# A hybrid decoder layer on one core: prompt scores in three split passes, square sums in two, two zero-fills dropped

## The chip, the cores and the metric

One core of one Trainium2 chip runs the whole layer as one program. The metric is device time in microseconds of one execution, as the median over executions. A program's executions differ a little, so two medians less than about 0.5% apart can't be told from no change here.

## What is computed

One inference step of one decoder layer (D_MODEL 2048) serves a prompt of 512 tokens and a sample group of 8 x 4 tokens with the same weights. Both groups stand side by side as 544 columns of the activations.

```
h = RMSNorm(x);  z = h @ W_in
branch A: sparse attention: compressed blocks, selected blocks, sliding window; 8 heads, 2 K/V groups
branch B: multi-scale causal pooling
branch C: Mamba-2 scan (16 heads of 64, state 128, chunks of 128), y * SiLU(z), then
          yg = yg * rsqrt(mean(yg*yg) + EPS)   over 2 groups of 512 channels
merge:    x + W_out( sum_b sigmoid(G_b) * (m_b @ W_branch_b) )
```

For the prompt, the selected-block and the window branch both see all earlier tokens (512 tokens are 8 selection blocks of 64, fewer than the 16 that are chosen, and the window is 512). So each is an ordinary causal softmax attention: scores `q k^T`, a causal mask, softmax, and a product with V. Everything is held in float32.

## The kernel before, in words

**Two ways of multiplying.** A plain float32 product is issued by the program as one call and runs as two instruction pairs (a weight load and a matmul, twice). The large projections instead split both operands into a rounded part `hi` and a remainder `lo`, both of the type float32r (`hsplit`, line 494: ScalarE writes `hi`, VectorE writes `lo`), and add three products, `hi*hi + lo*hi + hi*lo`. A float32r product runs as one instruction pair. All matmuls go through `mm` (L153), all ScalarE operations through `act` (L173), most of VectorE's through `tt`, `ts`, `stt` (L176, L181 and L182, L185), so the rows are told apart by their tiles' names.

**Units and sides.** `run_units` (line 462) goes through a list of units. A unit is a quarter of the contraction of one 128-column block of a projection: 24 float32r matmuls of 272 columns into the tile `zin`. With each unit it issues the weight loads of the unit six ahead and splits (`wh` on ScalarE, `wl` on VectorE) the weights of the unit three ahead. After each unit a counter decides whether the side work makes one step (0.55 steps per unit, later 0.75). Side work is a set of generators: attention, scan, norms. Below this program order a scheduler of the framework fixes the order on each engine by what is ready, so side matmuls stand between the matmuls of units.

**Tiles.** Most data tiles come from one pool, `U` (line 140), of 32 tiles of 128x608 float32. A tile goes back when the program lets go of it and its last reader is done. PSUM has four one-bank tiles (`A`, line 143) for side work and two pairs of banks for `zin`.

**Prompt attention**, `attn_p` (line 769), runs once for each K/V group g, one after the other, in the stretch from 396 to 718 us. It has 32 items (4 heads x 4 query blocks x 2 branches), two per step, in three stages that lag by a step each: `sa` (line 812) makes the scores of query block i against (i+1) x 128 keys, adds the causal mask on the last 128 columns by a bf16 product with the identity, and takes the softmax on VectorE and ScalarE (tile `P`); `sb` transposes P (tile `PT`, written back by VectorE or ScalarE in turn); `sc` multiplies with V (tile `O`). The 4 query tiles and the 2 key tiles of the group are let go at the end (lines 862 to 865).

**The scan**, `ssd` (line 1142), goes over 4 chunks. For each, `out(k)` (line 1183, k from 0 to 3) fills one PSUM tile `y` of two 128-column blocks e: a bf16 product of zeros (`zb`) over all 256 columns, then four heads (two per block, each on 64 of the 128 partitions; two instructions each), then for each block, from the second chunk on, the part that comes from the state (`yo`, two instructions), then a VectorE operation that reads the block.

**The group norm of the scan**, `m_norm` (line 1347), makes for each of 2 groups four tiles `mz`: it loads the gate, multiplies (VectorE) and squares (ScalarE). Then a product of an all-ones matrix with the four tiles sums over partitions into `ms`, in two halves of 272 columns, in plain float32: 8 products, 16 instruction pairs per group.

**Sample attention**, `samp_group` (line 1639): `begin` (line 1703) starts the tile `sO` with a bf16 product of zeros and adds the product of the new keys (`nt`, `vn`). It is called 8 times.

Of the kernel before, what the change touches and what calls it, by code (L numbers as in the profile page):

```python
# [8 lines left out]
R = mybir.dt.float32r  # L9
# [9 lines left out]
T = 544  # L19
NP = 512  # L20
H = 272
# [102 lines left out]
class Prog:  # L124
# [644 lines left out]
    def attn_p(s, g):  # L769
        nc = s.nc  # L770
        while not s.kv_done or s.turn != g:
            yield
        q = [s.qT[g * 4 + e] for e in range(4)]
        p = s.A("cs")
        for e in range(4):
            s.mm(p[32 * e:32 * e + 32, :NP], s.kcp[:, 32 * g:32 * g + 32], q[e][:, :NP])
        st = s.U("cst")
        s.act(st[:, :NP], p)
        yield
        p = s.A("ct")  # L780
        for i in range(4):
            s.tr(p[:, i * 128:i * 128 + 128], st[:, i * 128:i * 128 + 128])
        E = s.U("cE")
        e4 = E[:, :NP].rearrange("p (i h b) -> p i h b", i=4, h=4)
        s.tt(e4, p.rearrange("p (i h b) -> p i h b", i=4, h=4),
             s.c("cmpneg").rearrange("p (i b) -> p i b", i=4)[:, :, None, :].to_broadcast([128, 4, 4, 32]), OP.add)
        e3 = E[:, :NP].rearrange("p (x b) -> p x b", b=32)
        mx = s.small(16)
        nc.vector.tensor_reduce(mx, e3, axis=AX.X, op=OP.max)
        s.ts(mx, mx, -1e29, OP.max)  # L790
        s.tt(e3, e3, mx[:, :, None].to_broadcast([128, 16, 32]), OP.subtract)
        s.act(E[:, :NP], E[:, :NP], AF.Exp, scale=SC)
        yield
        sm = s.small(16)
        nc.vector.tensor_reduce(sm, e3, axis=AX.X, op=OP.add)
        s.ts(sm, sm, 1e-30, OP.max)
        nc.vector.reciprocal(sm, sm)
        gv = s.gn.rearrange("p i (h b) -> p i h b", b=3)
        s.tt(sm.rearrange("p (i h) -> p i h", i=4), sm.rearrange("p (i h) -> p i h", i=4),
             gv[:, :, g * 4:g * 4 + 4, 0])  # L800
        s.tt(e3, e3, sm[:, :, None].to_broadcast([128, 16, 32]))
        yield
        p = s.A("cpt")
        for i in range(4):
            s.tr(p[:, i * 128:i * 128 + 128], E[:, i * 128:i * 128 + 128])
        pc = s.U("pc")
        s.act(pc[:, :NP], p)
        yield
        us = [(e, br, i) for e in range(4) for i in range(4) for br in range(2)]
        PP, PT, OO = {}, {}, {}  # L810

        def sa(n):
            e, br, i = us[n]
            L = i * 128 + 128
            S = s.A("S")
            s.mm(S[:, :L], q[e][:, i * 128:L], s.kv[4 + 4 * br + g][:, :L], True, False)
            s.mm(S[:, L - 128:L], s.identb, s.trib, False, True)
            mx, sm = s.small(1), s.small(1)
            nc.vector.tensor_reduce(mx, S[:, :L], axis=AX.X, op=OP.max)
            s.ts(mx, mx, -1e29, OP.max, -SC, OP.mult)  # L820
            P = s.U("P")
            s.act(P[:, :L], S[:, :L], AF.Exp, bias=mx, scale=SC, accum_out=sm)
            s.ts(sm, sm, 1e-30, OP.max)
            nc.vector.reciprocal(sm, sm)
            c = (g * 4 + e) * 3 + 1 + br
            s.ts(P[:, :L], P[:, :L], sm, OP.mult, s.gn[:, i, c:c + 1], OP.mult)
            PP[n] = P

        def sb(n):
            i = us[n][2]  # L830
            P = PP.pop(n)
            L = i * 128 + 128
            t = s.A("PT")
            for kt in range(i + 1):
                s.tr(t[:, kt * 128:kt * 128 + 128], P[:, kt * 128:kt * 128 + 128])
            PT[n] = s.U("PT")
            if n % 2:
                s.act(PT[n][:, :L], t[:, :L])
            else:
                nc.vector.tensor_copy(PT[n][:, :L], t[:, :L])  # L840

        def sc(n):
            e, br, i = us[n]
            pt = PT.pop(n)
            if n % 8 == 0:
                OO[e] = s.A("O")
                s.mm(OO[e][:, :NP], s.vc4[32 * e:32 * e + 32, g], pc[32 * e:32 * e + 32, :NP], True, False,
                     skip_group_check=True)
            for kt in range(i + 1):
                s.mm(OO[e][:, i * 128:i * 128 + 128], s.Vn[kt][:, br * 256 + g * 128:br * 256 + g * 128 + 128],  # L850
                     pt[:, kt * 128:kt * 128 + 128], False, br == 1 and kt == i, skip_group_check=True)
            if n % 8 == 7:
                o = s.U("Os")
                s.act(o[:, :NP], OO.pop(e))
                nc.sync.dma_start(s.oT[g * 4 + e][:, :NP], o[:, :NP])
        for n in range(0, 36, 2):
            for f, d in ((sc, 4), (sb, 2), (sa, 0)):
                for m in (n - d, n - d + 1):
                    if 0 <= m < 32:
                        f(m)  # L860
            yield
        for e in range(4):
            del s.qT[g * 4 + e]
        for br in range(2):
            del s.kv[4 + 4 * br + g]
        s.turn = g + 1


# [273 lines left out]
    def ssd(s):  # L1142
        nc, a = s.nc, s.a
# [4 lines left out]
        for c in range(4):  # L1148
            cs = slice(c * 128, c * 128 + 128)
            xd, yo = [], []  # L1150
            for g in range(2):
                p = s.A("xn")
# [5 lines left out]
            p = s.A("bn")  # L1158
# [24 lines left out]
            def out(k):  # L1183
                E = ES.pop(k)
                g = k // 2
                p = s.A("y")
                s.mm(p[:, :256], s.zb[:, :128], s.zb, True, False, skip_group_check=True)
                for e in range(4):
                    x0 = ((k % 2) * 4 + e) * 64
                    s.mm(p[64 * (e % 2):64 * (e % 2) + 64, (e // 2) * 128:(e // 2) * 128 + 128], xd[g][:, x0:x0 + 64],  # L1190
                         E[:, e * 128:e * 128 + 128], False, c == 0, skip_group_check=True)
                for e in range(2):
                    if c:
                        x0 = ((k % 2) * 2 + e) * 128
                        s.mm(p[:, e * 128:e * 128 + 128], yo[g][:, x0:x0 + 128], s.c("ident"), False, True,
                             skip_group_check=True)
                    t = 2 * k + e
                    s.stt(s.xb[t][:, cs], s.xb[t][:, cs], s.dsk[:, t:t + 1], p[:, e * 128:e * 128 + 128],
                          OP.mult, OP.add)
# [3 lines left out]
            if c:  # L1203
                for g in range(2):
                    p = s.A("yo")
# [14 lines left out]
            for g in range(2):  # L1220
                s.tt(s.h64(xd[g][:, :NP]), s.h64(xd[g][:, :NP]), s.hb(s.dte[:, c, g * 8:g * 8 + 8]))
                p = s.A("st")
# [8 lines left out]
        for g in range(2):  # L1231
            p = s.A("fs")
# [114 lines left out]
    def m_norm(s):  # L1347
        nc = s.nc
        for t in range(8, 12):
            del s.xb[t]  # L1350
        for g in range(2):
            Z = []
            for e in range(4):
                y = s.xb[g * 4 + e]
                z = s.U("mz")
                nc.sync.dma_start(z[:, :T], s.mzd[g * 4 + e])
                s.tt(y[:, :T], y[:, :T], z[:, :T])
                s.act(z[:, :T], y[:, :T], AF.Square)
                Z.append(z)
            yield  # L1360
            P = [s.A("ms") for _ in range(2)]
            for e, z in enumerate(Z):
                for hf in range(2):
                    s.mm(P[hf][:, :H], s.c("ones"), z[:, hf * H:hf * H + H], e == 0, e == 3)
            del Z, z
            ss, rs, tmp = s.U("mss"), s.U("mrs"), s.U("mt")
            for hf in range(2):
                nc.vector.tensor_copy(ss[:, hf * H:hf * H + H], P[hf][:, :H])
            s.rsqrt(rs[:, :T], ss[:, :T], 0.25 / 512, tmp[:, :T])
            yield  # L1370
            for e in range(4):
                t = g * 4 + e
                y = s.xb.pop(t)
                s.stt(y[:, :T], y[:, :T], s.mnh[:, t:t + 1], rs[:, :T])
                nc.sync.dma_start(s.brd[16 + t], y[:, :T])
            yield
# [262 lines left out]
    def samp_group(s, q, oc, cnt, os_, CI, need):  # L1639
        nc, a = s.nc, s.a  # L1640
# [3 lines left out]
        for bl in range(2):  # L1644
            dst = a["o_win_s"][0, 2 * q + bl].rearrange("t k g d -> t (k g d)")
            for e in range(4):
                lo = 4 if e == 0 else 0
                nc.sync.dma_start(dst[e * 128 + lo - 4:e * 128 + 124], wn[bl, e][0][lo:, :NP])
        vn = s.U("vn")
# [3 lines left out]
        p = s.A("bq")  # L1653
        ql = s.qs[:, q].rearrange("p c w -> p (c w)")
# [47 lines left out]

        def begin(br, nt):
            po = s.A("sO")
            s.mm(po[:, :128], s.zb[:, :128], s.zb[:, :128], True, False, skip_group_check=True)
            s.mm(po[:, :128], nt[:16, :128], vn[:16, br * 128:br * 128 + 128], False, False, skip_group_check=True)
            return po

        def sums(po, pt, raw, o, last):
# [10 lines left out]
        p = s.A("vn")  # L1720
# [3 lines left out]
        p = scores(kT)  # L1724
# [10 lines left out]
        S = []  # L1735
        for lq in range(4):
            p = scores(kT)
# [20 lines left out]
        nt = news(0)  # L1758
# [282 lines left out]
```

## Time and profile before

| | |
|---|---|
| runs before | 2399.49 us median of 3 (2393.22 to 2402.33) |
| the profiled execution's own time | 2404.53 us |
| its span | 2402.8 us |
| instructions | 48653 |

The span is the time from the first to the last record of the profiled execution. Its own time is larger by 1.73 us, which lies around the span. Times within the trace are counted from the start of the span. In rows of the timeline the first number is the start, the second the length of the row; a matmul's length includes its way through the array, so what a matmul costs in a full queue is read from the start of one to the start of the next.

### The profile page before, as it was taken

How to read it: one execution, taken by the hardware profiler on the slowest of the kernel's cores; microseconds unless marked ns; L12 is line 12 of the kernel's file. 1: busy time of each engine (PE TensorE's matmuls, PEld its weight loads, DVE VectorE, ACT ScalarE, POOL GpSimd, SP SyncE). 2: the span in 40 equal slices, each digit the busy share in tenths (PEclk: the TensorE clock that was granted, in tenths of full speed). 3: DMA queues.
4: the chain of work that ended last, by engine and by line, in shares of the span. 5: the costliest groups of instructions: out<-in, count | busy, mean ns of one | idle time of the engine just before them, and what ended most of it. 6: DMA issues, size and time to landing. Idle time of an engine off the chain costs nothing.

```text
span 2402.8 us, 48653 instructions
## 1 busy us (share of the span) xinstructions
PE 2370.6 (99%) x19842; PEld 2247.1 (94%) x19842; DVE 1088.2 (45%) x2204; ACT 723.1 (30%) x1374; POOL 64.5 (3%) x157
## 2 busy tenths in 40 slices
PE   6999999999999999999999999999999999999999
PEld 6999898999999999989899989988899999999999
DVE  4326657554543322324544565665463344445222
ACT  4222323333333222322433342322242322223221
POOL 0001011000000000000001000000000000000000
PEclk8999999999999999999999999999999999999999
DMA  5775755545439798886587763345555654443442
GB/s 143 204 206 148 207 148 153 148 141 164 120 114 279 226 283 234 250 248 179 159 257 238 220 203 85 107 120 148 161 184 153 193 153 138 131 130 102 132 124 83
DMA packets 541201, 409.49 MB, mean 170 GB/s; under 512 B 26673, under 2 KB 472409, under 8 KB 540978
## 3 DMA queue, kind: packets, MB, share of 16 engines
q1 hardware_dynamic: 534066, 393.01, 56.4%
q10 hardware_dynamic: 6912, 13.37, 1.5%
q8 instruction: 156, 2.56, 0.5%
q14 instruction: 67, 0.55, 0.1%
HBM read 360.56 MB, written 113.21 MB: 197 GB/s over the span
## 4 chain that ended last, share of the span: by engine, by line
PE 94%; DVE 2%; DMA 2%; issue 1%; ACT 0%; POOL 0%; SPq 0%; DVEq 0%; ACTq 0%
PE zin L153 74%; PE kT L156 3%; PE O L153 2%; PE S L153 2%; PE xT L153 1%; PE y L153 1%; PE sO L153 1%; PE sS L153 1%; PE PT L156 1%; PE cS L153 1%; PE ns L153 1%; PE ocT L153 1%; DMA kr<-ckd 1%; PE qw L153 1%; DVE rp L176 1%
## 5 line engine op out<-in xcount | busy, mean ns | idle before, releaser
L176 DVE TENSOR_TENSOR wl<-wr,wh 128x512 fp32r<-128x512 f32 (+1 forms) x612 | 424.5, 694 | 889.6 <-ACT wh L173 887.6
L153 PE MATMUL zin<-hhi,wh 128*128 128x272 f32 (+2 forms) x3616 | 774.5, 294 | 0.0
L153 PE MATMUL zin<-hhi,wl 128*128 128x272 f32 (+2 forms) x3616 | 756.2, 289 | 4.3 <-DVE wl L176 4.3
L153 PE MATMUL zin<-hlo,wh 128*128 128x272 f32 (+2 forms) x3616 | 756.4, 290 | 0.0
L173 ACT ACTIVATE wh<-wr 128x512 fp32r<-128x512 f32 (+1 forms) x612 | 384.6, 628 | 1098.2 <-PE zin L153 1016.1
L153 PEld LDWEIGHTS zin<-hhi,wh 128*128 128x128 f32 (+1 forms) x3616 | 568.7, 188 | 24.1 <-issue 20.1
L153 PEld LDWEIGHTS zin<-hhi,wl 128*128 128x128 f32 (+1 forms) x3616 | 570.9, 189 | 8.3 <-DVE wl L176 5.0
L153 PEld LDWEIGHTS zin<-hlo,wh 128*128 128x128 f32 (+1 forms) x3616 | 567.7, 189 | 4.4 <-issue 3.5
L153 PE MATMUL zin<-bh,wh 128*128 128x272 f32 x1280 | 266.1, 289 | 1.5 <-DVE gt L185 1.5
L153 PE MATMUL zin<-bh,wl 128*128 128x272 f32 x1280 | 265.2, 288 | 0.0
L153 PE MATMUL zin<-bl,wh 128*128 128x272 f32 x1280 | 264.9, 288 | 0.0
L153 PEld LDWEIGHTS zin<-bh,wh 128*128 128x128 f32 x1280 | 200.3, 188 | 1.9 <-ACT bh L173 1.7
L153 PEld LDWEIGHTS zin<-bh,wl 128*128 128x128 f32 x1280 | 200.6, 188 | 0.0
L153 PEld LDWEIGHTS zin<-bl,wh 128*128 128x128 f32 x1280 | 200.4, 188 | 0.0
L156 PEld LDWEIGHTS kT<-cst,kr 128*128 128x128 f32 x512 | 55.7, 141 | 11.7 <-issue 10.1
L156 PE MATMUL kT<-cst,kr 128*128 128x128 f32 x512 | 65.1, 277 | 0.0
L173 ACT ACTIVATE mg<-zin 128x544 f32<-128x544 f32 x48 | 29.9, 624 | 112.8 <-PE zin L153 110.2
L173 ACT ACTIVATE kT<-kT 128x512 f32<-128x512 f32 x72 | 42.7, 596 | 55.8 <-PE kT L156 55.1
L1445 DVE COPY kT<-kT 128x512 f32<-128x512 f32 x72 | 48.2, 688 | 5.0 <-PE kT L156 4.6
L185 DVE SCALAR_TENSOR_TENSOR gt<-gt,zin 128x544 f32<-128x544 f32 x32 | 23.1, 721 | 48.1 <-PE zin L153 46.4
L173 ACT ACTIVATE P<-S,sm 128x128 f32<-128x128 f32 (+3 forms) x64 | 33.8, 528 | 36.8 <-DVE sm L182 22.8
L153 PE MATMUL S<-kv,q 128*128 128x128 f32 (+3 forms) x128 | 44.3, 450 | 0.0
(414 smaller groups left out, 1857.3 us busy)
## 6 DMA issues: line engine op xcount, KB each, us to landing
wr<-in_w_in_dram SPq DMA_DIRECT2D x224, 512.0 KB
ckd<-in_cache_kv_dram SPq DMA_DIRECT2D x256, 256.0 KB
kr<-ckd SPq DMA_DIRECT2D x256, 256.0 KB
wr<-in_w_branch_dram SPq DMA_DIRECT2D x48, 512.0 KB
wr<-in_w_out_dram SPq DMA_DIRECT2D x32, 512.0 KB
mgd<-mg ACTq DMA_DIRECT2D x48, 272.0 KB
gt<-mgd SPq DMA_DIRECT2D x48, 272.0 KB
cw<-in_cmp_w_dram SPq DMA_DIRECT2D x48, 256.0 KB
```

The lines of the kernel that those rows point to most:

```text
L153: return s.nc.tensor.matmul(out, l, r, start=start, stop=stop, **kw)
L156: return s.nc.tensor.transpose(out, in_, s.c("ident")[:k, :k])
L173: return s.nc.scalar.activation(out, in_, f, **kw)
L176: return (eng or s.nc.vector).tensor_tensor(out, a, b, op=op)
L185: return s.nc.vector.scalar_tensor_tensor(out, a, sc, b, op0=op0, op1=op1)
L1445: s.nc.vector.tensor_copy(u[:, :NP], p)
```

## The change

The prompt's scores are made by three products of split operands. `halves` splits a tile into `hi` and `lo` (two new tiles of the pool), and the unsplit tile is let go: both key tiles of the group and the first query tile ahead of the first item, each further query tile one step before its head's first item. In the scan the product of zeros goes, and the first head's product of each block half starts the sum; the order becomes two heads, state part, read, for each block. In the group norm the squares are split, the ones matrix is copied to float32r once, and the sums are made by two products (`hi` and `lo`). In the sample attention the product of zeros goes.

```diff
@@ attn_p
+        K, Q = {}, {}
+
+        def halves(v):
+            hi, lo = s.U("sh").bitcast(R), s.U("sl").bitcast(R)
+            s.hsplit(v[:, :NP], hi[:, :NP], lo[:, :NP])
+            return hi, lo
+
+        def query(e):
+            Q[e] = halves(s.qT.pop(g * 4 + e))
+        for br in range(2):
+            K[br] = halves(s.kv.pop(4 + 4 * br + g))
+        query(0)
 
         def sa(n):
             e, br, i = us[n]
             L = i * 128 + 128
             S = s.A("S")
-            s.mm(S[:, :L], q[e][:, i * 128:L], s.kv[4 + 4 * br + g][:, :L], True, False)
+            (qh, ql), (kh, kl) = Q[e], K[br]
+            for n_, (a_, b_) in enumerate(((qh, kh), (ql, kh), (qh, kl))):
+                s.mm(S[:, :L], a_[:, i * 128:L], b_[:, :L], n_ == 0, False)
             s.mm(S[:, L - 128:L], s.identb, s.trib, False, True)
...
+        q = None
         for n in range(0, 36, 2):
+            if n % 8 == 0 and 0 < n < 32:
+                Q.pop(n // 8 - 1)
+            if n % 8 == 6 and n < 24:
+                query(n // 8 + 1)
             for f, d in ((sc, 4), (sb, 2), (sa, 0)):
...
             yield
-        for e in range(4):
-            del s.qT[g * 4 + e]
-        for br in range(2):
-            del s.kv[4 + 4 * br + g]
         s.turn = g + 1
@@ ssd, out(k)
                 p = s.A("y")
-                s.mm(p[:, :256], s.zb[:, :128], s.zb, True, False, skip_group_check=True)
-                for e in range(4):
-                    x0 = ((k % 2) * 4 + e) * 64
-                    s.mm(p[64 * (e % 2):64 * (e % 2) + 64, (e // 2) * 128:(e // 2) * 128 + 128], xd[g][:, x0:x0 + 64],
-                         E[:, e * 128:e * 128 + 128], False, c == 0, skip_group_check=True)
                 for e in range(2):
+                    for e_ in (2 * e, 2 * e + 1):
+                        x0 = ((k % 2) * 4 + e_) * 64
+                        s.mm(p[64 * (e_ % 2):64 * (e_ % 2) + 64, e * 128:e * 128 + 128], xd[g][:, x0:x0 + 64],
+                             E[:, e_ * 128:e_ * 128 + 128], True, c == 0, skip_group_check=True)
                     if c:
                         x0 = ((k % 2) * 2 + e) * 128
                         s.mm(p[:, e * 128:e * 128 + 128], yo[g][:, x0:x0 + 128], s.c("ident"), False, True,
@@ m_norm
                 s.act(z[:, :T], y[:, :T], AF.Square)
-                Z.append(z)
+                hi, lo = s.U("mzh").bitcast(R), s.U("mzl").bitcast(R)
+                s.hsplit(z[:, :T], hi[:, :T], lo[:, :T])
+                Z.append((hi, lo))
+            hi = lo = z = None
+            if g == 0:
+                on = s.U("on").bitcast(R)
+                nc.vector.tensor_copy(on[:, :128], s.c("ones"))
             yield
             P = [s.A("ms") for _ in range(2)]
-            for e, z in enumerate(Z):
+            for e in range(4):
                 for hf in range(2):
-                    s.mm(P[hf][:, :H], s.c("ones"), z[:, hf * H:hf * H + H], e == 0, e == 3)
-            del Z, z
+                    for j in range(2):
+                        s.mm(P[hf][:, :H], on[:, :128], Z[e][j][:, hf * H:hf * H + H], e == 0 and j == 0, e == 3 and j == 1)
+            Z = None
@@ samp_group, begin
             po = s.A("sO")
-            s.mm(po[:, :128], s.zb[:, :128], s.zb[:, :128], True, False, skip_group_check=True)
-            s.mm(po[:, :128], nt[:16, :128], vn[:16, br * 128:br * 128 + 128], False, False, skip_group_check=True)
+            s.mm(po[:, :128], nt[:16, :128], vn[:16, br * 128:br * 128 + 128], True, False, skip_group_check=True)
             return po
```

## Rows read from the trace of the kernel before

**Rows 1.** The page, busy time and share of the span of each engine.
```profile
PE 2370.6 (99%) x19842; PEld 2247.1 (94%) x19842; DVE 1088.2 (45%) x2204; ACT 723.1 (30%) x1374; POOL 64.5 (3%) x157
```

**Rows 2.** Waits of PE over the whole run, the longest: total, times, longest.
```profile
PE xT L153 <- DVE dg L181: 12.3, 3, 8.2
```

**Rows 3.** Windows: length, busy PE, PEld, DVE, ACT, POOL, clock, DMA; attention group 0, scan.
```profile
396.00:550.00 154.00, 152.97 (x1141) 138.98 (x1140) 80.99 (x223) 54.09 (x126) 3.02 (x3) 1.00 0.48 139
...
1550.00:1645.00 95.00, 95.00 (x725) 82.06 (x724) 64.10 (x159) 23.89 (x42) 1.02 (x3) 1.00 0.38 104
```

**Rows 4.** The tile S, matmuls of the scores: ns min/median/max, first and last start.
```profile
L153 PE MATMUL S<-kv,q x128: 272/460/649, 397.0 to 703.2; 128*128 128x128 f32 x32, 128*128 128x256 f32 x32, 128*128 128x384 f32 x32, 128*128 128x512 f32 x32
```

**Rows 5.** Timeline of PE: scores of 512 and of 128 columns, with what follows.
```profile
454.88 1.02 PE L153 MATMUL S<-kv,q 128*128 128x512 f32 x2
455.74 0.22 PE L153 MATMUL S<-trib,identb 128*128 128x128 bf16 x1
...
465.04 0.39 PE L153 MATMUL S<-kv,q 128*128 128x128 f32 x2
465.26 0.22 PE L153 MATMUL S<-trib,identb 128*128 128x128 bf16 x1
```

**Rows 6.** Timeline of PE: float32r products of 256 columns at the start.
```profile
22.04 0.28 PE L153 MATMUL zin<-hhi,wh 128*128 128x256 f32 x1
...
22.97 0.28 PE L153 MATMUL zin<-hlo,wh 128*128 128x256 f32 x1
```

**Rows 7.** The chain that ended last: a stretch of float32r products of 272 columns.
```profile
2375.31 12.05 PE zin L153 x96
```

**Rows 8.** Timeline of PE: twelve float32 instructions of 128 columns in a row.
```profile
462.83 1.50 PE L153 MATMUL O<-PT,Vn 128*128 128x128 f32 x12
464.16 1.04 PE L156 MATMUL PT<-cst,P 128*128 128x128 f32 x8
```

**Rows 9.** Timeline of PE: the group norm's sums and the unit behind them.
```profile
1738.45 3.83 PE L153 MATMUL ms<-mz,cst 128*128 128x272 f32 x16
...
1742.36 0.41 PE L153 MATMUL zin<-hhi,wl 128*128 128x272 f32 x2
```

**Rows 10.** Timeline of PE: the sample attention's sO started.
```profile
1165.39 0.23 PE L153 MATMUL sO<-zb 128*128 128x128 bf16 x1
1165.55 0.48 PE L153 MATMUL sO<-vn,nT 16*128 16x128 f32 x2
```

**Rows 11.** Timeline of PE: the scan's y, in the first and the second chunk.
```profile
1552.89 0.28 PE L153 MATMUL y<-zb 128*128 128x256 bf16 x1
1553.10 0.66 PE L153 MATMUL y<-E,xd 128*64 128x128 f32 x8
1553.69 0.28 PE L153 MATMUL y<-zb 128*128 128x256 bf16 x1
...
1578.27 0.49 PE L153 MATMUL y<-cst,yo 128*128 128x128 f32 x2
1578.69 0.43 PE L153 MATMUL y<-E,xd 128*64 128x128 f32 x2
1579.05 0.49 PE L153 MATMUL y<-cst,yo 128*128 128x128 f32 x2
1579.29 0.50 PE L153 MATMUL zin<-hhi,wh 128*128 128x272 f32 x2
```

**Rows 12.** Timeline of PEld (weight loads) in the same place, idle before it in brackets.
```profile
1579.05 0.30 PEld L153 LDWEIGHTS y<-cst,yo 128*128 128x128 f32 x2 [0.17 <-issue]
```

**Rows 13.** Splits of a 128x512 tile, by line and form: count, busy, mean ns, idle before.
```profile
L173 ACT ACTIVATE wh<-wr 128x512 fp32r<-128x512 f32 x608 | 383.1, 630 | 1091.0 <-PE zin L153 1010.8 <-issue 72.9 <-DMA ckd<-in_cache_kv_dram 2.4
L176 DVE TENSOR_TENSOR wl<-wr,wh 128x512 fp32r<-128x512 f32 x608 | 423.0, 697 | 879.6 <-ACT wh L173 877.6 <-DMA wr<-in_w_in_dram 1.3
```

**Rows 14.** Timeline of PE: the first scores of group 0 and their first transpose.
```profile
396.96 0.38 PE L153 MATMUL S<-kv,q 128*128 128x128 f32 x2
...
402.30 0.33 PE L156 MATMUL PT<-cst,P 128*128 128x128 f32 x1 [1.01 <-DVE sm L181]
```

## The prediction

> **What bounds the kernel now.** I read the page first: PE is busy for 2370.6 of 2402.8 us, VectorE for 45% and ScalarE for 30% [rows 1]. Then PE's waits: the longest entry is 12.3 us in the opening, where the change does nothing [rows 2]. Then the busy time of the stretches that the change touches. In the attention of group 0 (that of group 1 is alike) and in the scan PE is busy for all but 1 us, at a granted clock of 1.00, while VectorE has about half of the attention free and a third of the scan, and ScalarE two thirds or more [rows 3]. So the time is the length of PE's queue. What an edit is worth is how much earlier the next matmul starts, and work on other engines costs only what it makes PE wait for. A matmul's own length in a row is no measure of that; starts are.
>
> **The prices of a pass.** A float32 score product of 512 columns holds the queue for 0.86 us in its two instructions (454.88 to 455.74), one of 128 columns for 0.22 (465.04 to 465.26) [rows 5]; that is one price per column, so 384 columns cost 0.645 and 256 cost 0.43. A float32r instruction of 272 columns costs 12.05/96 = 0.1255 us [rows 7], of 256 columns 0.93/8 = 0.116 us (22.04 to 22.97) [rows 6]. At 2.4 GHz and a column per cycle these stream in 0.113 and 0.107, so a pass costs its columns plus some 0.01 us: I take 0.225 at 512 columns, 0.172 at 384, 0.118 at 256. At 128 columns the trace has no float32r product. From below it is 0.065 (0.053 of streaming plus 0.012); from above the price of a whole float32 product of that width, 0.22. The nearest row is float32 instructions of the same width with as large a weight load, 1.33/12 = 0.111 us (462.83 to 464.16) [rows 8]; I take that.
>
> The Trainium skill ("TensorE: Matmul & The Clock Gate", LDWEIGHTS) gives a weight load as columns over 1.2, about 107 ns for 128 columns whatever the product's width. By that rule a narrow product is bound by its load and three loads lose to two. By an estimate from it three passes at 128 columns cost 0.32 us, and the sum below would gain 0.2 us more. The trace's 0.111 agrees with it, but a float32 stream of 128 columns takes as long, so the row doesn't decide it.
>
> **Scores.** The 128 score instructions are 64 products, 16 of each width [rows 4]. Three passes against one float32 product: 512 columns 0.86 - 0.68 = 0.18 saved, 384 columns 0.645 - 0.516 = 0.13, 256 columns 0.43 - 0.354 = 0.076, 128 columns 0.22 - 0.333 = 0.11 lost. Sum 0.276, times 16: **4.4 us saved**. The good end, passes at pure streaming plus 2 ns for the wide ones (0.215, 0.162, 0.109) and 0.065 for the narrow one, is 0.215 + 0.159 + 0.103 + 0.025 = 0.50, 8.0 us saved. The bad end, 0.22 for each narrow pass, is 0.9 us lost.
>
> The splits come on top: 6 per group of 128x512, 0.63 us on ScalarE and 0.70 on VectorE each [rows 13], 12 in all. They add 3.8 and 4.2 us to each attention stretch; in group 0's, ScalarE is free for 100 of 154 us and VectorE for 73 [rows 3]. Later query tiles are split a step ahead of their use, with one to two units of 24 x 0.1255 = 3.0 us between. The three at the start stand directly ahead of the first scores; queue order on ScalarE puts weight splits `wh` behind them and on VectorE `wl`, for units three ahead. Their operands were final well before, and the scheduler can place them in idle time, so I cost them at nothing. If that cover is gone, PE waits 3 x 0.63 + 0.70 = 2.6 us once per group, 5.2 us. No DMA moves.
>
> **Group norm.** 16 float32 instructions hold PE from 1738.45 to 1742.11 (the unit pair's second start 1742.36 less one pair of 0.25), 0.229 each [rows 9]; the change issues as many float32r ones at 0.1255. 32 x 0.103 = **3.3 us saved**, 3.0 to 3.4. The 8 splits (of 544 columns, by the rate of 512 [rows 13] 0.67 and 0.74 us each) and one copy lengthen the way from gate to sum by 1.4 us per tile. Units of the next projection cover them, and nothing but the sums waits for them; if each group's four were exposed in a row it would be 2 x 4 x 1.4 = 11 us.
>
> **Sample start.** A product of zeros takes 0.16 us of the queue (1165.39 to 1165.55) [rows 10], 8 times 1.3 us. Part of that is the change of weights behind a narrow tile, which the next product inherits: at least 0.053 of streaming goes. I take 0.11, **0.9 us saved** (0.4 to 1.3).
>
> **Scan.** Here the order costs what the dropped product saves. The zeros cost 0.21 us to the next start, four heads 0.59, one head 0.36; the state part costs 0.24 when a unit follows and 0.42 when heads follow [rows 11]. Two 64-partition heads evidently run side by side, 0.21 us per pair of heads, and each switch from heads to a full-width product leaves 0.16 us, in which the load of the next weights waits (0.17) [rows 12]. So a call from the second chunk on costs 0.21 + 0.59 + 2 x 0.24 = 1.28 before, up to 1.37 with the state part at 0.33 once. After: twice (0.37 for two heads, 0.24 to 0.42 for the state part) plus 0.10 to enter from a unit: 1.32 to 1.68, I take 1.45. That is 0.13 lost, with ends 0.05 saved and 0.35 lost, 12 times: 1.5 us lost. In the first chunk there is no state part; 0.80 becomes 0.59 plus 0.10 or 2 x 0.37 plus an entry: 0.1 saved, 4 times 0.4. Together **1.1 us lost** (1.4 saved to 4.6 lost). VectorE's read of block 0 now stands between the heads of the two blocks and shares the bank with the second, so block 1's heads wait for it; before, block 1's state part did. Units fill that gap.
>
> The Trainium skill ("TensorE: Matmul & The Clock Gate", Part 3) has weight loads overlap running matmuls only where their row groups differ. By it every change between heads and state part is exposed, which speaks against this order: by an estimate from it the scan stands at its bad end and the whole saving is 3.5 us smaller. The idle 0.17 us ahead of that load agrees [rows 12].
>
> **Sum.** 4.4 + 3.3 + 0.9 - 1.1 = 7.5 us saved, against the profiled execution's 2404.53: 2397.0. That execution is 5.0 us above the median of the runs, so the same saving there gives 2399.5 - 7.5 = **2392.0 us**. All good ends together save 14.1 us, all bad ends lose 2.0.
>
> **Rivals.**
> - *Narrow passes cost a float32 product.* Nothing in the trace shows a float32r product under 256 columns. Then the scores lose 0.9 instead of saving 4.4, and the time is 2397.3. For: no row excludes it. Against: three times the nearest row's rate of 0.111 already covers a full load. Chance 0.13.
> - *Passes overlap fully.* The 0.01 us above streaming vanishes at 384 and 512 columns and narrow loads hide, with the scan's order rearranged by the scheduler: 14.1 saved, 2385.4. For: no row has a float32r product of 384 or 512 columns, and a longer stream leaves a load more room. Against: 96 products in a row all show the extra [rows 7]. Chance 0.19.
> - *Slower: the tile pool runs out.* The group's two key tiles become four until its end, and a query tile becomes two: three tiles more at the start, four while two heads are split, none net only from the fourth head. By my count from the code group 0 stands at 29 of 32 now (8 query, 4 key and 4 value tiles, up to 6 of P and PT, 7 others). Above 32 the softmax's P or PT waits for a tile of the step before, and the lag that hides it is gone. The chain from first scores to first transpose is 5.3 us (396.96 to 402.30) [rows 14]; a unit covers 3.0. With 2.3 to 5.3 us exposed in each of the first 8 steps it costs 18 to 42 us, with 30 in the middle: 2422. Against: PE loses 1 us in that stretch now [rows 3], and unit work can be moved up. Chance 0.12.
>
> That the splits do nothing is no case: the instruction counts are fixed by the code.
>
> **How the numbers follow.** The forecast has 0.56, with its own range 2386 to 2399: its sum's ends and the runs' own spread. 0.5% is 12.0 us, about what a measurement of this kernel can tell from no change. Faster by more than that takes all good ends, 0.19, or the forecast's lower edge with a kind order of the scheduler, 0.05: 0.24. Slower by more takes the pool, 0.12. The rest, 0.64, is within 0.5%. The range 2382 to 2404 takes in the first two rivals with the spread of runs and leaves out the pool and a remainder.
>
> **What would show it.** In the changed profile: scores of 512 columns at 0.67 us from first start to mask and of 128 at 0.33; the norm's sums at 0.125 each; no `zb` in `sO` and one in `y`; two heads, then state part, at 1.4 us per call; PE still at 99%, its waits in the attention under 3 us. Wrong would be: PE waits on splits `sl` or on P in the first eight steps; narrow passes at 0.2; or a saving outside these three stretches, which my sum doesn't hold.

## The result, and the profile after

The changed kernel takes **2415.95 us** (median of 7 runs, 2408.62 to 2418.35); the kernel before took 2401.53 us beside it (7 runs). The ratio is **1.0058** with a 95% interval of 1.0047 to 1.0070: slower by 0.58%, some 14 us. The forecast was 2392.0, its range ended at 2404. The intervals here and below rest on 4 to 29 runs of each kernel, so some of them tell differences under the half per cent named at the start.

The page of the changed kernel, busy time of each engine (the answer to [rows 1]) and PE's clock in 40 slices:

```profile
PE 2364.0 (98%) x19882; PEld 2247.0 (93%) x19882; DVE 1101.6 (46%) x2225; ACT 734.6 (31%) x1394; POOL 64.6 (3%) x157
...
PEclk9999999999999999999999999999989999999999
```

PE is busy for 6.6 us less than before, in a span that is 5.1 us longer (2407.9): it stands idle for longer. How much of the 6.6 is less work can't be read here, for the opening, in which PE is busy too, was 4.9 us shorter in this execution (the table below). PE's waits over the whole run say what it waits for (the answer to [rows 2]; total, times, longest):

```profile
PE xT L153 <- DVE dg L181: 11.6, 3, 7.5
PE ms L153 <- ACT mzh L173: 7.6, 3, 4.2
PE zin L153 <- ACT mg L173: 6.4, 2, 3.8
...
PE ms L153 <- DVE on L1379: 0.7, 1, 0.7
...
PE S L153 <- DVE sl L176: 0.6, 1, 0.6
```

The opening's entry (`xT`) is the old one. New are the sums of the group norm (`ms`) waiting for a split square (`mzh`), and a unit in the same place waiting for an eviction (`mg`). In the attention, where the slow rival was expected, the splits cost a wait of 0.6 us.

**Where the time went, by marks.** The opening's length differs between executions of any kernel (the first score came at 391.9 to 404.3 us in the thirteen profiled ones below), so I read marks behind it: the first score, the last start of the scan's last `y` product (`yq`), the first product of the branch projections (`zin<-bh`), and the span's end. All but the end are first and last starts in the rows of the tiles `S`, `y` and `bh`.

| kernel | first score | last `yq` | first `bh` | `yq` to `bh` | first score to end |
|---|---|---|---|---|---|
| before | 397.0 | 1734.1 | 1905.2 | 171.1 | 2005.8 |
| changed | 392.1 | 1720.9 | 1910.1 | 189.2 | 2015.8 |
| norm undone | 396.4 | 1725.6 | 1896.6 | 171.0 | 1997.8 |
| norm alone | 397.6 | 1731.8 | 1922.0 | 190.2 | 2021.9 |
| loads first | 392.8 | 1722.2 | 1890.1 | 167.9 | 1994.9 |
| batched | 401.0 | 1730.3 | 1898.2 | 167.9 | 1994.5 |
| pairs taken first | 404.3 | 1733.0 | 1922.0 | 189.0 | 2015.2 |
| split after | 396.6 | 1725.6 | 1893.5 | 167.9 | 1994.2 |
| scores alone | 399.4 | 1728.8 | 1899.8 | 171.0 | 1997.6 |
| scan alone | 400.4 | 1736.8 | 1907.9 | 171.1 | 2005.1 |
| sample alone | 396.6 | 1731.1 | 1902.1 | 171.0 | 2004.3 |
| batched, four starts | 397.4 | 1722.0 | 1889.9 | 167.9 | 1989.4 |
| batched, two starts | 391.9 | 1716.0 | 1883.9 | 167.9 | 1989.1 |

Two corrections belong to it. Every kernel with the new scores issues 2286 projection products ahead of the first score instead of 2256 (counts of PE's groups in that window). Those 30 x 0.1255 = 3.8 us are moved, not saved; add them where such a kernel's last column is compared with the kernel before. And some 2.3 us of the kernel before's last column belong, as far as these traces tell, to this one execution: from the first score to the scan's first `y` product it takes 1155.9 us, while norm alone and scan alone, whose instructions on PE are the same up to there, take 1153.6 and 1153.7. It waits 1.0 us for the softmax (`PT`) where those two wait 0.3, and the rest builds up at the products that read cache rows (`pv`).

Of the stretches between the marks that of the norm is the only one that got longer by more than 0.2 us: 189.2 us against 171.1. In windows (length; busy PE, PEld, DVE, ACT, POOL; clock; DMA share, GB/s), first the changed kernel, then the kernel before around the same work:

```profile
1726.00:1775.00 49.00, 35.15 (x249) 33.02 (x247) 27.04 (x39) 20.41 (x29) 0.00 (x0) 0.87 0.46 138
...
1750.00:1753.00 3.00, 0.48 (x2) 0.48 (x3) 3.00 (x5) 1.31 (x2) 0.00 (x0) 0.50 0.47 147
1753.00:1756.00 3.00, 3.00 (x17) 3.00 (x17) 1.51 (x3) 0.00 (x0) 0.00 (x0) 0.57 1.01 341
```

```profile
1726.00:1765.00 39.00, 39.00 (x271) 36.41 (x271) 26.57 (x39) 16.27 (x23) 0.00 (x0) 1.00 0.39 123
```

PE had no gap there before; now it is idle for 13.85 of 49 us, and the clock stands at 0.50 (the 1.2 GHz level) in the longest gap and for a while after it.

**How it came.** Before, SP issues the four gate loads of a group in one go, and the eight are out before the first result is stored. SP's queue of the kernel before:

```profile
1718.15 1.99 SPq L1356 DMA_DIRECT2D mz<-mzd  x4
...
1737.46 2.00 SPq L1356 DMA_DIRECT2D mz<-mzd  x4
...
1752.97 2.41 SPq L1375 DMA_DIRECT2D brd<-xb  x4
```

SP's queue of the changed kernel (the load is now L1370, the store L1396):

```profile
1730.62 0.37 SPq L489 DMA_DIRECT2D wr<-in_w_in_dram  x1
1731.09 0.53 SPq L1370 DMA_DIRECT2D mz<-mzd  x1
1736.95 0.37 SPq L489 DMA_DIRECT2D wr<-in_w_in_dram  x1
1737.42 0.54 SPq L1370 DMA_DIRECT2D mz<-mzd  x1
...
1751.81 2.45 SPq L1396 DMA_DIRECT2D brd<-xb  x4
1754.35 0.41 SPq L1370 DMA_DIRECT2D mz<-mzd  x1
1760.70 0.38 SPq L489 DMA_DIRECT2D wr<-in_w_in_dram  x1
1761.14 1.04 SPq L1370 DMA_DIRECT2D mz<-mzd  x2
```

The first five stand each alone behind a weight load, 6 to 10 us apart. Only the first of group 1's four (1737.42) goes out ahead of group 0's stores; the other three stand behind them, and the stores wait for group 0's norm on VectorE. So in group 1 the chain of a tile (load, product, square, split, sum) runs once for each tile, one after the other, and group 0's sums start 17.8 us behind the last `yq` (1738.66) instead of 4.3 (1738.45 before). PE's queue shows what that makes of the sums:

```profile
1752.52 0.82 PE L153 MATMUL ms<-mzh,on 128*128 128x272 f32 x2 [4.15 <-ACT mzh L173]
...
1753.36 0.66 PE L153 MATMUL zin<-hhi,wh 128*128 128x272 f32 x2
1753.82 0.66 PE L153 MATMUL zin<-hhi,wl 128*128 128x272 f32 x2
...
1756.35 0.41 PE L153 MATMUL zin<-hhi,wl 128*128 128x272 f32 x2
...
1768.06 0.52 PE L153 MATMUL ms<-mzh,on 128*128 128x272 f32 x2 [2.04 <-ACT mzh L173]
...
1770.89 0.82 PE L153 MATMUL ms<-mzh,on 128*128 128x272 f32 x2 [1.45 <-ACT mzh L173]
...
1776.23 0.82 PE L153 MATMUL zin<-hhi,wh 128*128 128x272 f32 x2 [3.76 <-ACT mg L173]
```

The first of these gaps is that of the tile whose load was early: its product stands on VectorE behind group 0's norm, at 1750.37, much as before (1751.53). But before, PE had units from 1742.36 to the next sums at 1754.14 to fill this with; now 36 products stand there, 4.5 us. That the late loads changed the order of the whole stretch, and this gap with it, is read from the kernels below, in which it is gone.

Behind the gap of 4.15 us a pair of instructions takes 0.46 us (1753.36 to 1753.82), and 0.25 again from 1756.35 on. Not every gap does this: behind that of 2.65 us, ahead of it, the granted clock was 1.00 and a pair took 0.25 us from the second on (1747.07 to 1747.32). The gaps of the stretch add to 15 us; counted pair by pair, the 1.2 GHz level behind them costs about 4 more. Against the kernels whose loads stand together the stretch is 189.2 - 167.9 = 21.3 us longer; 0.6 of that are five more projection products that fell into it, and under 2 us I can't place.

The waits on `mg` are a second effect in the same place. On ScalarE, ahead of the first of them (2.65 us):

```profile
1743.04 0.66 ACT L173 ACTIVATE mrs<-mss 128x544 f32<-128x544 f32 x1
1744.10 0.63 ACT L173 ACTIVATE wh<-wr 128x512 fp32r<-128x512 f32 x1 [0.40 <-PE zin L153]
1744.75 1.28 ACT L173 ACT_TABLE_LOAD   x1
1746.04 0.62 ACT L173 ACTIVATE mg<-zin 128x544 f32<-128x544 f32 x1
```

The eviction that frees `zin` stands behind the norm's square root, a weight split and a table load. The same operations stand there in the kernel before, and PE doesn't wait for them.

**The parts that were forecast.** Scores of 512 and of 128 columns on PE (the answer to [rows 5]):

```profile
411.61 0.48 PE L153 MATMUL S<-sh,sh 128*128 128x512 f32 x1
411.93 0.39 PE L153 MATMUL S<-sh,sl 128*128 128x512 f32 x1
412.16 0.40 PE L153 MATMUL S<-sl,sh 128*128 128x512 f32 x1
412.39 0.23 PE L153 MATMUL S<-trib,identb 128*128 128x128 bf16 x1
...
455.53 0.30 PE L153 MATMUL S<-sh,sh 128*128 128x128 f32 x1
455.67 0.28 PE L153 MATMUL S<-sh,sl 128*128 128x128 f32 x1
455.79 0.27 PE L153 MATMUL S<-sl,sh 128*128 128x128 f32 x1
455.90 0.23 PE L153 MATMUL S<-trib,identb 128*128 128x128 bf16 x1
```

From the first start to the mask 0.78 and 0.37 us, where 0.68 and 0.33 were expected. The second and third pass of 512 columns take 0.23 each, where 0.225 was assumed; the first, entered from a float32 product, 0.32. A narrow pass takes 0.14, 0.12, 0.11.

The norm's sums (the answer to [rows 9]), 16 instructions from 1738.66 to 1740.77 where the unit goes on: 0.23 for the first and 0.125 for each other, as forecast:

```profile
1738.66 0.39 PE L153 MATMUL ms<-mzh,on 128*128 128x272 f32 x1 [0.73 <-DVE on L1379]
1738.89 0.29 PE L153 MATMUL ms<-mzl,on 128*128 128x272 f32 x1
...
1740.77 0.29 PE L153 MATMUL zin<-hlo,wh 128*128 128x272 f32 x1
```

A call of the scan from the second chunk on (the answer to [rows 11]), 1561.93 to 1563.33 = 1.40 us:

```profile
1561.93 0.44 PE L153 MATMUL y<-E,xd 128*64 128x128 f32 x4
1562.30 0.49 PE L153 MATMUL y<-cst,yo 128*128 128x128 f32 x2
1562.71 0.44 PE L153 MATMUL y<-E,xd 128*64 128x128 f32 x4
1563.08 0.49 PE L153 MATMUL y<-cst,yo 128*128 128x128 f32 x2
1563.33 0.50 PE L153 MATMUL zin<-hhi,wh 128*128 128x272 f32 x2
```

### The profile page after: what moved, and what is told of

Its sections match the earlier page's. It is cut to its first block, busy times and chain, and to the rows that moved or that the text cites. A ratio compares the mean times of both kernels' runs of the same rounds, so it can differ in the third digit from the quotient of the medians.

```text
span 2407.9 us, 48794 instructions
## 1 busy us (share of the span) xinstructions
PE 2364.0 (98%) x19882; PEld 2247.0 (93%) x19882; DVE 1101.6 (46%) x2225; ACT 734.6 (31%) x1394; POOL 64.6 (3%) x157
## 4 chain that ended last, share of the span: by engine, by line
PE 93%; DVE 3%; DMA 2%; ACT 1%; issue 1%; SPq 0%; POOL 0%; DVEq 0%; ACTq 0%
PE zin L153 74%; PE kT L156 3%; PE O L153 2%; PE S L153 2%; PE y L153 1%; DMA wr<-in_w_in_dram 1%; PE sO L153 1%; PE sS L153 1%; PE cS L153 1%; PE PT L156 1%; PE ns L153 1%; DVE wl L176 1%; PE xT L153 1%; PE ocT L153 1%; PE pv L153 1%; PE qw L153 1%
## 5 line engine op out<-in xcount | busy, mean ns | idle before, releaser
L153 PEld LDWEIGHTS O<-PT,Vn 128*128 128x128 f32 x320 | 38.5, 191 | 6.1 <-issue 6.1
```

The lines of the kernel that those rows point to most:

```text
L153: return s.nc.tensor.matmul(out, l, r, start=start, stop=stop, **kw)
```

## The experiments

**Which part does it.** Theory: the order of the norm's loads. Rivals: the scores, the scan's order, or the split work itself. First the changed kernel without its edits of the norm, and the kernel before with these alone.

```diff
@@ m_norm of the changed kernel
-                hi, lo = s.U("mzh").bitcast(R), s.U("mzl").bitcast(R)
-                s.hsplit(z[:, :T], hi[:, :T], lo[:, :T])
-                Z.append((hi, lo))
+                Z.append(z)
```

Norm undone: 

> The changed kernel with the group norm of before; scores, scan and sample start stay changed. Theory (the whole loss sits in the group norm: four gate loads that come one by one and a chain of two engines per tile leave TensorE idle for some 17 us there, and its clock falls): faster than before by 3 to 8 us, ratio 0.997 to 0.9985, no wait on mzh or mg, granted clock 0.995 or above in that stretch. Rival (the loss is spread: splits of the scores and the scan's order cost as well): no faster than before, ratio 1.000 or above.

Norm alone: 

> The kernel before with only the group norm changed. Theory (the loss is the norm's own): slower than before by 15 to 22 us, ratio 1.006 to 1.009, with the same waits of TensorE on mzh and mg. Rival (the norm suffers only because the earlier edits brought it earlier or filled the tile pool): within 4 us of before.

Norm undone measured 2399.95 us, ratio 0.9988 (0.9979 to 0.9997), just above the 0.997 to 0.9985 expected. The waits on `mzh` and `mg` are gone, and SP issues the loads four at a time (1709.63, 1728.94). Norm alone measured 2421.32, ratio 1.0078 (1.0065 to 1.0092), with 7.0 us of waits on `mzh` and 6.4 on `mg`. The norm's edits are the whole loss; the rest of the change costs nothing, and by the runs saves a little.

**Is it the loads' order, or the split?** The four loads of a group in a loop of their own ahead, and everything else as changed; then the norm in three loops over its four tiles (loads; products and squares; splits).

```diff
@@ loads first
+            zs = []
+            for e in range(4):
+                zs.append(s.U("mz"))
+                nc.sync.dma_start(zs[e][:, :T], s.mzd[g * 4 + e])
             for e in range(4):
...
-                z = s.U("mz")
-                nc.sync.dma_start(z[:, :T], s.mzd[g * 4 + e])
+                z, zs[e] = zs[e], None
```

Loads first: 

> The changed kernel, with the four gate tiles of a group taken and loaded ahead of the first split; the multiply, square and split of each tile follow one after the other as in the change. Theory (tiles of the pool are handed out in program order, so the next gate tile and its load come only after the split tiles of the one before): the loads of a group stand together on the load queue again, ahead of the stores of the group before, the waits on mzh fall from 7.6 us to under 3, and the time is 2385 to 2400. Rival (the alternation of the two engines within a tile is what takes the time): loads together but waits on mzh still 5 us or more, time within 4 us of the changed kernel.

Batched: 

> As the run with the loads first, and besides all four multiplies and squares of a group stand ahead of its splits. Theory (late loads): no more than 3 us faster than with the loads first, 2385 to 2398 us. Rival (alternation): 8 us or more faster than with the loads first.

Loads first measured 2397.87, ratio 0.9988 (0.9977 to 0.9999); batched 2396.16, ratio 0.9967 (0.9957 to 0.9977). In both the eight splits are still there, the loads stand together, no wait on `mzh` or `mg` is left, and the stretch from `yq` to `bh` takes 167.9 us. So the split work is covered, as the forecast had it, as long as the loads are early.

**What puts the loads apart.** I had first put it down to the pool: a load's tile is handed out behind the two tiles of the split before it. Two kernels tell this from the load's place in the program.

```diff
@@ pairs taken first
-            Z = []
+            Z = [(s.U("mzh").bitcast(R), s.U("mzl").bitcast(R)) for _ in range(4)]
...
-                hi, lo = s.U("mzh").bitcast(R), s.U("mzl").bitcast(R)
+                hi, lo = Z[e]
@@ split after
                 s.act(z[:, :T], y[:, :T], AF.Square)
+                zs.append(z)
+            for e in range(4):
+                z = zs[e]
                 hi, lo = s.U("mzh").bitcast(R), s.U("mzl").bitcast(R)
```

Pairs taken first: 

> The changed kernel with the eight tiles of a group's halves taken ahead of the loop, the loads left in it. Theory A, the hand-out of tiles: a load's tile is taken behind the two tiles of the split before it and can't be issued until that split is placed; with the pairs taken first the four gate loads of a group stand together on SP's queue again, PE's waits on mzh go, and the time is that of the loads-first run, 2398 us (ratio .9988). Theory B, the place of the load behind the split's two instructions: nothing about the order changes, loads one by one between the weight loads, three loads of group 1 behind group 0's stores, waits on mzh of 7 us and on mg of 6 us, and 2416 us (ratio 1.0058).

Split after: 

> The changed kernel with the four splits of a group in a second loop; load, product and square stay in the first, each load in the loop. Theory B, the place of the load behind the split: the four loads stand together (about 0.5 us each on SP) ahead of the stores of group 0, no wait on mzh, and 2398 us as with the loads first (ratio .9975 to 1.0). Rival, the work of the split itself (eight more instructions of ACT and DVE in a group) costs the time wherever the load stands: waits on mzh or mzl of several us stay, and 2410 us or more (ratio 1.003 and up).

Pairs taken first measured 2418.03, ratio 1.0067 (1.0048 to 1.0086), with the changed kernel's waits, and its loads go out one by one again, three of them behind the stores:

```profile
PE zin L153 <- ACT mg L173: 6.4, 2, 3.8
PE ms L153 <- ACT mzh L173: 6.1, 3, 2.9
```

```profile
1749.00 0.53 SPq L1370 DMA_DIRECT2D mz<-mzd  x1
...
1763.30 2.46 SPq L1395 DMA_DIRECT2D brd<-xb  x4
1765.85 1.30 SPq L1370 DMA_DIRECT2D mz<-mzd  x1
```

Split after measured 2396.88, ratio 0.9978 (0.9967 to 0.9989). SP's queue of that kernel:

```profile
1709.62 1.99 SPq L1370 DMA_DIRECT2D mz<-mzd  x4
...
1728.98 1.96 SPq L1370 DMA_DIRECT2D mz<-mzd  x4
...
1742.92 2.41 SPq L1399 DMA_DIRECT2D brd<-xb  x4
```

Here each load is in the loop as in the changed kernel, and no split stands between two loads. That the order in which tiles are handed out does it falls with the first kernel; the load's place in the program behind the split of the tile before is what both agree with. One more difference no run separates from it: the changed kernel and pairs first let go of a gate tile between two loads, the three kernels with early loads only behind all four. And why the scheduler holds a load back behind a split, and not behind the product and the square that stood there before, these runs don't tell either.

**The other parts alone**, each put into the kernel before (as in the change's diff, that part alone).

Scores: 

> The kernel before with only the prompt's scores changed. By the rows of the changed profile a pass of 512 columns takes 0.232 us, not the 0.225 I took, and the first pass behind a float32 product some 0.09 more, so three passes save 0.1 us at 512 and 0.05 at 384 columns, nothing at 256, and lose 0.1 at 128. Theory (switching between float32 and float32r products eats the gain): within 2 us of before. Rival (the sum on record): 4 us faster.

Scan: 

> The kernel before with only the scan changed: no product of zeros, two heads and state part per block. Theory (two more switches between heads and state part per call cost what the zeros cost): 0 to 3 us slower than before. Rival (the zeros were worth their whole 0.21 us): 3 us faster.

Sample start: 

> The kernel before without the product of zeros that starts the sample attention's sum. Theory: 0.4 to 1.3 us faster, which lies within the noise of five rounds; the trace shows 8 starts less of 0.16 us each. Rival (the following product inherits the wait of the weight load): the next product of the tile takes longer by as much, nothing saved.

Scores alone measured 2398.07, ratio 0.9984 (0.9975 to 0.9992), 2 to 6 us saved. By marks it is 2005.8 - 1997.6 = 8.2, less the 3.8 moved ahead and the 2.3 of that one execution of the kernel before: 2.1. Summed over all starts of the attention, the products save only 1.0 us and the mask loses 1.7 until the next start, but the 160 transposes of P, which now follow other neighbours, take 2.4 us less; that makes 1.7. From the first score to the first `y` it takes 1148.2 + 3.8 = 1152.0 us against 1153.6 and 1153.7 in norm alone and scan alone, 1.6 and 1.7 less. So the traces bear out "within 2 us", and the runs' 2 to 6 reach over it; they hold the opening too, which marks leave out. Scan alone measured 2402.45, ratio 1.0002 (0.9990 to 1.0015): from the first `y` to the last `yq` it takes 182.7 us against 181.2, with 832 projection products between in both, so the order costs 1.5 us more than the zeros did. Sample alone measured 2399.75, ratio 0.9990 (0.9981 to 0.9999). At its eight places, from the start ahead of the tile to the start behind these products, 7.2 us became 6.3.

**A better version.** The batched norm, and in the scan all four heads ahead of the two state parts; in a second kernel with a start on the first head of each partition half alone.

```diff
@@ out(k): heads first
                 p = s.A("y")
+                for e in range(4):
+                    x0 = ((k % 2) * 4 + e) * 64
+                    s.mm(p[64 * (e % 2):64 * (e % 2) + 64, (e // 2) * 128:(e // 2) * 128 + 128], xd[g][:, x0:x0 + 64],
+                         E[:, e * 128:e * 128 + 128], True, c == 0, skip_group_check=True)
@@ two starts
-                         E[:, e * 128:e * 128 + 128], True, c == 0, skip_group_check=True)
+                         E[:, e * 128:e * 128 + 128], e < 2, c == 0, skip_group_check=True)
```

Four starts: 

> The changed kernel with the norm batched (all loads, then all multiplies and squares, then the splits) and the scan without zeros but in the order of before: all four heads, then the state parts. Theory (the order of the scan costs 2 to 4 us): 2 to 4 us faster than the batched run with the scan as changed, 2392 to 2395 us, and one switch from heads to state part per call in the trace. Rival (the scheduler fills the switches anyway): the same as that run.

Two starts: 

> The norm in three passes over its four tiles (as in the batched run), and in the scan the four heads' products of a call ahead of its two state products, with a fresh start on the first head of each partition half alone (heads 0 and 1), the other two adding. Theory: a start clears what both blocks of the tile hold in its half, so the first two products begin both blocks and the sum is whole; one change of shape less per call, 24 calls x .16 us = 3.9 us, as in the run with four starts: about 2391 us, ratio .9945 to .997 to the kernel before. Rival: the four starts themselves were the gain there: then 2396 as the batched run, ratio .9967.

With four starts 2391.01, ratio 0.9954 (0.9941 to 0.9967), some 5 us under the batched kernel's 2396.16 where 2 to 4 were expected. The Trainium skill ("PSUM — Partial Sum Buffer", Terms, Zero region) has a start make the whole bank of the written partitions begin anew, not its own columns alone. By that rule block 1's starts reach block 0, and this kernel leaves block 0's heads out of its sum from the second chunk on, with the same instructions; no trace here shows a bank's content. With two starts 2391.16, ratio **0.9957** (0.9941 to 0.9974): faster than both kernels. Its interval reaches over the batched kernel's, so what the order is worth beside that one is told by marks: 1989.1 against 1994.5. Heads and state part of a call of the scan in it:

```profile
1566.11 0.66 PE L153 MATMUL y<-E,xd 128*64 128x128 f32 x8
1566.70 0.49 PE L153 MATMUL y<-cst,yo 128*128 128x128 f32 x2
```

The scheduler still mixes calls, but eight instructions of heads (four heads) go through in 0.59 us (1566.11 to 1566.70) instead of twice 0.37, and from the first `y` to the last `yq` the scan takes 177.84 us against the batched kernel's 182.75: 4.9 us, 3.9 forecast (the 24 calls of that sum are 12, with two changes of shape less in each). With four starts it is 177.8 too, so the rival, that the starts themselves were the gain, falls.

## Why the prediction was wrong

- **The step that failed** is in the group norm: "Units of the next projection cover them, and nothing but the sums waits for them", beside a "No DMA moves" that stood for the scores and was never asked of the norm. The prediction took the norm's loads to stay where they were, and no row of it looks at the norm's stretch on SP, VectorE or ScalarE. The split's own 1.4 us per tile is covered: with early loads PE has no wait on `mzh`. What moved was the gate loads: they stand in the loop behind the split of the tile before, came apart on SP's queue, and three slid behind stores that wait for the other group. It is 21.3 us by marks, 1.0058 against 0.9967 to 0.9988 for the three kernels whose loads stand together. The text priced the tiles of both groups exposed in a row at 11 us as a bound and then left that out of "all bad ends", as it did the 5.2 us of the scores' splits; measured, it was twice the 11, with 15 us of gaps and about 4 of the lower clock in it.
- **The rest of the sum came out smaller in the traces.** 7.5 us were to be saved. The batched kernel has every edit and its loads together: 0.9967 (0.9957 to 0.9977) is 5.5 to 10.3 us by runs. By marks 2005.8 - 1994.5 - 3.8 = 7.5, but 2.3 of that belong to the one execution of the kernel before, which leaves 5.2; the four terms below add to 4.3. That 7.5 came out of one pair of executions is luck, and which of these figures is nearest stays open.
- *Group norm, 3.3 saved*: 171.1 - 167.9 = 3.2 in every kernel with early loads and the split.
- *Scores, 4.4 saved*: this term was mis-sized; it is 1.7 in the traces. Per product the saving against the old mean from start to start (0.89, 0.675, 0.46, 0.27 at 512, 384, 256, 128 columns) is 0.10, 0.06, 0.01 and -0.10, less than forecast at the three wider ones, since the first pass behind a float32 product costs up to 0.09 us more. The mask and the transposes, which the sum didn't hold, add 0.7 net.
- *Scan, 1.1 lost*: 1.5 lost between its marks; the call at 1.40 us is near the 1.45 forecast, and the bad end of 4.6 lost didn't come. The prediction's estimate had put the scan there by half of what the Trainium skill ("TensorE: Matmul & The Clock Gate", Part 3) states: the same part also has loads into a background weight buffer pulled ahead. The trace agrees: 96 products in a row, with as many weight loads as products [rows 1], start 0.1255 us apart [rows 7], 0.01 over their streaming.
- *Sample start, 0.9 saved*: 0.9 at its eight places (7.2 to 6.3), 0.2 to 4.6 by runs.
- **The rivals.** Narrow passes at 0.11 to 0.14 us are far from 0.22, so that one falls. Passes don't overlap fully either: 0.23 at 512 columns. The tile pool did not run out in the attention: PE waits 0.6 us on `sl` and 0.2 on the softmax (`sm`) there. The slow outcome had its chance, 0.12, on the wrong place.
- **What would show it.** Right: no `zb` in `sO` and one in `y`, the sums at 0.125, two heads and state part at 1.4 us per call, attention waits under 3 us. Missed: scores at 0.78 and 0.37 us instead of 0.67 and 0.33. Wrong: PE at 98% and waits in the norm, for which the text named no sign at all.

## What to carry to other kernels

A load that a loop issues is part of the price of whatever is put ahead of it in the next turn: after adding work inside a loop, look for the loop's loads in the DMA-issuing queue, what stands between them and which store they fall behind. Where a chain of load, compute and sum is repeated, write all loads first; here that alone is 21 us, and writing the steps in passes as well adds nothing that the marks show (1994.9 and 1994.5). And a bound that the text works out (11 us) belongs in the range until a row shows the cover.

## What the runs showed that was not expected

- A gap on PE can cost more than itself: behind one of 4.15 us a pair of products took 0.46 us instead of 0.25 for about 3 us, at a granted clock of 0.50 to 0.57; behind one of 2.65 us the clock stayed at 1.00.
- A float32r pass of 512 columns costs 0.32 us behind a float32 product and 0.23 behind another float32r pass. One of 128 columns costs 0.14 behind another kind of product and 0.11 to 0.12 behind another such pass.
- The scheduler of the framework changes a queue's order with what is written between two transfers, even where no operand connects them: the same eight loads came in two groups of four or one by one.
- One profiled execution can hold 2.3 us that others of the same instructions don't, as that of the kernel before does; a part worth 2 us has to be weighed against more than one trace.
